# RMS norms of a two-layer backbone: squares added up as channel tiles finish, means by one-column matmuls inside the matmuls that follow

## The chip, the cores and the metric

The kernel runs on one core of one Trainium2 chip. The metric is the time of one execution on the device in microseconds, the median of several runs. A core has TensorE (PE, matmuls), VectorE (DVE), ScalarE (ACT), GpSimd (POOL) and SyncE (SP, which here only issues DMA transfers). Each engine takes its instructions in a fixed order and waits by semaphores for what the others make.

## What is computed

The reference is a backbone of two layers over 512 latent tokens and 256 context tokens with 1024 channels. A layer is

```
h = modulate(rms_norm(x, n1))                # per stream: latents, context
y = merge(conv(h), attention(h), deltanet(h))
x = x + gate1 * (y @ w_o)                    # output projection
h = modulate(rms_norm(x, n2))
x = x + gate2 * (convffn(h) @ f_dn)

rms_norm(x, g) = x * rsqrt(mean(x * x over channels) + 1e-6) * g
modulate(h)    = h * (1 + scale) + shift
```

Everything is float32. Only the latents are the output, so the last layer's context part stops early: its second norm and FFN are done for latents alone.

## The kernel before

Channels lie on partitions: a stream is eight tiles of 128 channels by its tokens, latents `l` with 512 columns and context `c` with 256. A mean over channels is therefore a sum over partitions and over eight tiles. Every large matmul is made of three products of exact high and low parts (`whi`, `wlo` for weights, `hl`/`ol` and `hc`/`oc` for modulated latents and context, `zhl`/`zol` and `zhc`/`zoc` for the merged branches). A weight unit (`wunit`, L140 to L152) is one DMA on SP's queue into one of two `raw` buffers, a cast to `whi` on ACT (L150) and a subtraction to `wlo` on DVE (L151); `ahead` prepares the next unit while one is used. A unit with eight channel tiles is 24 matmuls (`mm_b`, L169).

Eight norms are computed with `norm_stat` (L293 to L317): two at the start (before layer 0), latents' and context's second norm of layer 0 (behind `out_proj`), latents' and context's first norm of layer 1 (behind the last `down` of layer 0's FFN), and the second norm of layer 1, in two halves of 256 latents. For each of eight tiles ACT squares the tile (`sq`, L300) and PE multiplies the squares by a constant of 32 equal columns (`nps`, L302), four groups of 32 rows of a PSUM bank adding two tiles each. ACT copies the bank (`npe`, L304), four further matmuls add the groups and put a quarter of the tokens on each 32 rows (L307), DVE adds eps (`ms`, L310) and takes the reciprocal root in eleven operations (`_rsqrt`, L56 to L61: `nrt`, `nry`) on 128 or 64 columns, and four matmuls spread the result over all partitions (`nrb`, L314). `norm_apply` gives eight closures, one a channel tile: DVE scales (`nt`, L323), ACT adds the shift and rounds (L334), DVE makes the low part (L335).

In `out_proj` the loop runs over two parts (latents, then context; in the last layer two halves of latents) and in each over eight output tiles `m`; behind a tile's matmuls (`wo`) DVE adds the residual (`xml`, `xmc`, L1212) with a tile `xo` that is loaded through SP. The first part's norm is emitted behind its loop, and its eight closures are emitted one behind each tile of the second part's loop. While the first part runs, each tile emits instead a step of the modulation (`ada_steps`): loads of tables (`at`, SP, L262) and products on DVE (`aj`, L275). The last `down` of layer 0 is built in the same way, with residuals in `x`; the second part's norm and closures come behind the loop. The first unit of the FFN (`up(0)`) runs its three weight units over the first part and then over the second, so that the second part's norm can lie beside the first part's matmuls. Layer 1 begins with output-gate matmuls with tokens on the columns of the result (`og_proj`, L177, four groups of latents and then the context's 16 columns).

The order on each engine is set by a scheduler that walks the program in its order of emission, with pools of buffers (tags `t0` and `t1` have two buffers each; `sq`, `nt` and `aj` share `t1`) and with `issue_after`, which holds a closure behind a given instruction.

Of the kernel before, what the change touches and what calls it, by code (L numbers as in the profile page):

```python
# [31 lines left out]
# amounts of independent work emitted between dependent stages  # L32
# [3 lines left out]
# columns of the packed constants  # L36
# [3 lines left out]
# columns of the packed per-layer parameters  # L40
# [8 lines left out]
def _rsqrt(nc, sm, x, n, name):  # L49
    """1/sqrt(x) for a [128, n] tile: a seed from the exponent, then Newton steps to float32."""  # L50
# [14 lines left out]
class Net:  # L65
    def __init__(self, tc, A, out):
        self.tc, self.nc, self.A, self.out = tc, tc.nc, A, out
        self.queue, self.live, self.primed = deque(), None, None

    # ---------------------------------------------------------------- set-up  # L70
# [69 lines left out]
    # ---------------------------------------------------------------- weights  # L140
# [13 lines left out]
    def ahead(self, src, n, cols):  # L154
        """the weight units src(0) .. src(n - 1), each prepared while the one before is used"""
# [6 lines left out]
    def mm_b(self, outs, w, xs):  # L162
        """outs[s] = sum_k w(k).T @ xs[s][k], w and xs as exact (high, low) parts."""
        n = len(xs[0])
        for k in range(n):
            wk = w(k)
            for i, (a, b) in enumerate(((0, 0), (0, 1), (1, 0))):
                for o, x in zip(outs, xs):
                    self.nc.tensor.matmul(o, wk[a], x[k][b], start=(k == 0 and i == 0), stop=(k == n - 1 and i == 2))  # L169

    def mm_a(self, o, x, w):
        """o = sum_k x[k].T @ w(k), tokens on partitions."""
# [12 lines left out]
    # ---------------------------------------------------------------- adaLN  # L185
# [11 lines left out]
    def ada_rows(self):  # L197
        """silu(c) and silu(c_ctx) on every partition"""
# [88 lines left out]
    # ---------------------------------------------------------------- modulated RMSNorm  # L287
    def new_h(self, streams=(("l", NL), ("c", NX))):
        return {s: [self.pair_tiles(s, k) for k in range(8)] for s, _ in streams}

    def norm_stat(self, x, part):
        """1/rms of the tokens [a, b) of a stream, on every partition (a PSUM bank)"""
        nc, kc = self.nc, self.kc  # L293
        s, a, e = part
        n = e - a
        q = n // 4
        ps = self.bank("nps")
        for k in range(8):
            sq = self.tp.tile([128, 512], F32, tag="t1", name="sq")
            nc.scalar.activation(sq[:, :n], x[s][k][:, a:e], AF.Square)  # L300
            g = 32 * (k % 4)
            nc.tensor.matmul(ps[g:g + 32, :n], kc[:, K_S1024:K_S1024 + 32], sq[:, :n], start=k < 4, stop=k >= 4)  # L302
        pe = self.tp.tile([128, 512], F32, tag="t0", name="npe")
        nc.scalar.copy(pe[:, :n], ps[:, :n])  # L304
        p2 = self.bank("nps2")
        for g in range(4):
            nc.tensor.matmul(p2[32 * g:32 * g + 32, :q], kc[:, K_S32:K_S32 + 32], pe[:, q * g:q * g + q],  # L307
                             start=True, stop=True)
        ms = self.sm.tile([128, 128], F32, tag="ms", name="ms", bufs=1)
        nc.vector.tensor_scalar(ms[:, :q], p2[:, :q], EPS, None, ALU.add)  # L310
        r = _rsqrt(nc, self.sm, ms[:, :q], q, "nr")
        rb = self.bank("nrb")
        for g in range(4):
# [1100 lines left out]
```

## Time and profile before

| | us |
|---|---|
| median of 3 runs | 2627.74 |
| lowest, highest | 2625.46, 2634.8 |
| span of the profiled execution | 2622.8 |
| PE busy in it | 2530.2 (96%) |
| DVE busy | 1834.8 (70%) |
| ACT busy | 1071.1 (41%) |

The profile is one execution, with each instruction's start, its length, and the idle time of its engine before it with what ended that. Matmuls overlap in their pipeline, so two starts tell more than one length: the pace is the difference of starts. The granted clock (PEclk) is a share of TensorE's full speed. PE is near full all through the span, in 40 slices 9 tenths or more in all but the first and two others.

### The profile page before, as it was taken

How to read it: one execution, taken by the hardware profiler on the slowest of the kernel's cores; microseconds unless marked ns; L12 is line 12 of the kernel's file. 1: busy time of each engine (PE TensorE's matmuls, PEld its weight loads, DVE VectorE, ACT ScalarE, POOL GpSimd, SP SyncE). 2: the span in 40 equal slices, each digit the busy share in tenths (PEclk: the TensorE clock that was granted, in tenths of full speed). 3: DMA queues.
4: the chain of work that ended last, by engine and by line, in shares of the span. 5: the costliest groups of instructions: out<-in, count | busy, mean ns of one | idle time of the engine just before them, and what ended most of it. 6: DMA issues, size and time to landing. Idle time of an engine off the chain costs nothing. (4 is left out here: it accounts for less than half of the span.)

```text
span 2622.8 us, 42526 instructions
## 1 busy us (share of the span) xinstructions
PE 2530.2 (96%) x16247; PEld 2150.7 (82%) x16247; DVE 1834.8 (70%) x4082; ACT 1071.1 (41%) x2166; POOL 8.4 (0%) x32
## 2 busy tenths in 40 slices
PE   7999999999989999999999999998999999999999
PEld 3989888977878868888888788887887778888887
DVE  5676578789579968776656467776778976755463
ACT  3464343454332244223223345634354543533242
POOL 0000000000000000000000000000000000000000
PEclk8999999999999999999999999998999999999999
DMA  7224434352458643453432333343446375333332
GB/s 246 90 79 130 135 95 144 99 194 95 170 175 267 194 136 120 123 159 119 150 127 89 113 123 102 119 130 114 146 125 209 107 246 173 122 92 101 96 97 89
DMA packets 207276, 356.78 MB, mean 136 GB/s; under 512 B 54832, under 2 KB 103200, under 8 KB 206944
## 3 DMA queue, kind: packets, MB, share of 16 engines
q1 hardware_dynamic: 182176, 320.97, 39.1%
q10 hardware_dynamic: 24896, 33.09, 3.6%
q8 instruction: 128, 2.10, 0.3%
q14 instruction: 76, 0.62, 0.1%
HBM read 297.31 MB, written 56.68 MB: 135 GB/s over the span
## 5 line engine op out<-in xcount | busy, mean ns | idle before, releaser
L151 DVE TENSOR_TENSOR wlo<-raw,whi 128x1024 fp32r<-128x1024 f32 (+2 forms) x320 | 386.9, 1210 | 303.4 <-ACT whi L150 300.6
L150 ACT CAST whi<-raw 128x1024 fp32r<-128x1024 f32 (+2 forms) x320 | 332.5, 1040 | 626.5 <-PE dn L169 197.2
L169 PE MATMUL upl<-ol,whi 128*128 128x512 f32 (+1 forms) x728 | 282.3, 388 | 0.0
L169 PE MATMUL upl<-hl,whi 128*128 128x512 f32 (+1 forms) x728 | 282.1, 388 | 0.0
L169 PE MATMUL upl<-hl,wlo 128*128 128x512 f32 (+1 forms) x728 | 280.6, 386 | 0.7 <-DVE wlo L151 0.7
L454 PE MATMUL pjl<-hl,whi 128*128 128x512 f32 x512 | 210.9, 412 | 7.6 <-ACT whi L150 7.6
L525 DVE SCALAR_TENSOR_TENSOR ca<-yp,caw,ca 128x783 f32<-128x783 f32 (+1 forms) x240 | 213.0, 888 | 7.4 <-ACT ca L518 4.6
L454 PE MATMUL pjl<-hl,wlo 128*128 128x512 f32 x512 | 206.2, 403 | 0.9 <-DVE wlo L151 0.9
L454 PE MATMUL pjl<-ol,whi 128*128 128x512 f32 x512 | 206.2, 403 | 0.0
L169 PEld LDWEIGHTS upl<-ol,whi 128*128 128x128 f32 x728 | 136.8, 188 | 32.6 <-issue 2.1
L169 PEld LDWEIGHTS upl<-hl,wlo 128*128 128x128 f32 x728 | 136.8, 188 | 31.3 <-issue 1.2
L169 PEld LDWEIGHTS upl<-hl,whi 128*128 128x128 f32 x728 | 136.7, 188 | 29.1 <-issue 1.2
L169 PE MATMUL dn<-fhl,wlo 128*128 128x512 f32 x352 | 139.0, 395 | 0.0
L169 PE MATMUL dn<-fll,whi 128*128 128x512 f32 x352 | 139.0, 395 | 0.0
L169 PE MATMUL dn<-fhl,whi 128*128 128x512 f32 x352 | 138.6, 395 | 0.3 <-DVE xml L1280 0.3
L454 PEld LDWEIGHTS pjl<-hl,whi 128*128 128x128 f32 x512 | 97.7, 191 | 29.2 <-ACT whi L150 9.7
L275 DVE CUSTOM_DVE_ANT_1 aj<-at,crows,par 128x512 f32<-128x512 f32 x128 | 92.9, 749 | 34.1 <-DMA at<-ada_t 21.3
L454 PEld LDWEIGHTS pjl<-hl,wlo 128*128 128x128 f32 x512 | 97.5, 191 | 21.9 <-DVE wlo L151 1.6
L454 PEld LDWEIGHTS pjl<-ol,whi 128*128 128x128 f32 x512 | 98.2, 192 | 19.1 <-issue 0.5
L590 PE MATMUL na<-wlo,hl 128*128 128x256 f32 x384 | 108.8, 284 | 0.6 <-DVE wlo L151 0.6
L590 PE MATMUL na<-whi,hl 128*128 128x256 f32 x384 | 109.1, 285 | 0.0
L590 PE MATMUL na<-whi,ol 128*128 128x256 f32 x384 | 109.0, 284 | 0.0
(390 smaller groups left out, 6461.0 us busy)
## 6 DMA issues: line engine op xcount, KB each, us to landing
raw<-w_b SPq DMA_DIRECT2D x88, 512.0 KB
raw<-f_up SPq DMA_DIRECT2D x88, 512.0 KB
at<-ada_t SPq DMA_DIRECT2D x160, 256.0 KB
raw<-w_o SPq DMA_DIRECT2D x32, 512.0 KB
raw<-f_dn SPq DMA_DIRECT2D x32, 448.0 KB
raw<-w_a SPq DMA_DIRECT2D x24, 512.0 KB
mg<-mge ACTq DMA_DIRECT2D x48, 256.0 KB
raw<-w_br SPq DMA_DIRECT2D x24, 512.0 KB
```

The lines of the kernel that those rows point to most:

```text
L150: self.nc.scalar.copy(hi[:, :n], r[:, :n])
L151: self.split = self.nc.vector.tensor_sub(lo[:, :n], r[:, :n], hi[:, :n]).ins
L169: self.nc.tensor.matmul(o, wk[a], x[k][b], start=(k == 0 and i == 0), stop=(k == n - 1 and i == 2))
L275: V.tensor_tensor_reduce(p, w, self.crows[:, r, 4 * h:4 * h + 4], 1.0, m if h else self.p(l, "adab")[:, t:t + 1], ALU.mult, ALU.add, accum ...
L454: self.nc.tensor.matmul(o, wk[a], x[k][b], start=(k == 0 and i == 0), stop=(k == n - 1 and i == 2))
L525: nc.vector.scalar_tensor_tensor(a, y[:, k:k + n], w[:, 31 * c + k:31 * c + k + 1], a, ALU.mult, ALU.add)
L590: self.nc.tensor.matmul(ps[:, :256], x[k][a], wk[b], start=(k == 0 and j == 0), stop=(k == 7 and j == 2))
```

## The change

`norm_stat` is cut in pieces. `norm_open` takes a running tile `nac` for a part; `norm_add` squares a finished channel tile on ACT (the first square goes into `nac` itself) and adds it to `nac` on DVE (new line L306); it is called in the loops of `out_proj` and of the last `down`, right behind each tile's residual. `norm_mean` multiplies each block of 128 tokens of `nac`, as stationary operand, by one constant column (L314 after), so that a token's mean lands on its own partition, in one column for each block; eps and the reciprocal root then work on four or two columns. `norm_row` spreads them: a matmul for each block of 128 tokens, with a column of the root repeated 128 times as stationary operand and the identity as moving one (L324 after). The copy `npe` and the second step are gone.

The list of closures now holds the mean, then the spreading with the first two tiles, then six tiles. The first part's list is taken up one entry a tile in the second part's loop, as before. The second part's list is kept in `self.late`: `up(0)` emits the mean behind channel tile 6 of its first unit, the spreading behind tile 4 of the second, the rest behind tile 0 of the third (`mm_b` has a new argument `then`); in layer 1 `og_proj` emits the mean behind its first group and the rest behind its second, and the close of a pool (`zes`) has moved there from the layer's start. Every closure of `norm_apply` is still held behind `self.split`, now also when it is emitted late; mean and spreading are not. Comments and docstrings are gone too.

```
+    def norm_open(self, part):
+        n = part[2] - part[1]
+        return {"n": n, "k": 0, "acc": self.tp.tile([128, 512], F32, tag="t0", name="nac")[:, :n]}
+
+    def norm_add(self, st, x):
+        nc, n = self.nc, st["n"]
+        if st["k"] == 0:
+            nc.scalar.activation(st["acc"], x, AF.Square)
+        else:
+            sq = self.tp.tile([128, 512], F32, tag="t1", name="sq")[:, :n]
+            nc.scalar.activation(sq, x, AF.Square)
+            nc.vector.tensor_add(st["acc"], st["acc"], sq)
+        st["k"] += 1
+
+    def norm_mean(self, st):
+        nc, nt = self.nc, st["n"] // 128
+        ps = self.bank("nps")
+        for t in range(nt):
+            nc.tensor.matmul(ps[:, t:t + 1], st["acc"][:, 128 * t:128 * t + 128], self.kc[:, K_S1024:K_S1024 + 1],
+                             start=True, stop=True)
+        ms = self.sm.tile([128, 4], F32, tag="ms", name="ms")
+        nc.vector.tensor_scalar(ms[:, :nt], ps[:, :nt], EPS, None, ALU.add)
+        st["r"] = _rsqrt(nc, self.sm, ms[:, :nt], nt, "nr")
+
+    def norm_row(self, st):
+        rb = self.bank("nrb")
+        for t in range(st["n"] // 128):
+            self.nc.tensor.matmul(rb[:, 128 * t:128 * t + 128], st["r"][:, t:t + 1].to_broadcast([128, 128]), self.ident,
+                                  start=True, stop=True)
+        st["rb"] = rb
...
-    def norm_apply(self, l, x, h, part, rb, gain, shift):
+    def norm_apply(self, l, x, h, part, st, gain, shift):
...
+        def head():
+            self.norm_row(st)
+            one(0)
+            one(1)
+
+        return [lambda: self.norm_mean(st), head] + [lambda k=k: one(k) for k in range(2, 8)]
...
@@ og_proj
+                if i == 0 and t == 2:
+                    for f in self.late[:1]:
+                        f()
+                elif i == 0 and t == 3:
+                    for f in self.late[1:]:
+                        f()
+                    self.zes.close()
...
@@ out_proj, in the loop over m
+                self.norm_add(st, self.x[s][m][:, a:e])
...
-            late = self.norm_apply(l, self.x, self.h, part, self.norm_stat(self.x, part), g2, 3)
-        for f in late:
-            f()
+            late = self.norm_apply(l, self.x, self.h, part, st, g2, 3)
+        self.late = late
...
@@ up(0)
+                    mean, head, *rest = self.late
+                    then = [{6: mean}, {4: head}, {0: lambda: [f() for f in rest]}]
                     for part in self.parts():
                         for u in us:
-                            self.up_mm(*u, [part])
+                            self.up_mm(*u, [part], then.pop(0) if then else {})
...
@@ the last down
-                        down(k0, k1, hid, [p], self.xsrc, late)
-                        late = self.norm_apply(l + 1, self.x, self.h, p, self.norm_stat(self.x, p), g1, 0)
-                    for f in late:
-                        f()
+                        st = self.norm_open(p)
+                        down(k0, k1, hid, [p], self.xsrc, late, st)
+                        late = self.norm_apply(l + 1, self.x, self.h, p, st, g1, 0)
+                    self.late = late
```

On PE, at the end of layer 0's latent output projection and the beginning of the context's, the order before is (`wo` is the projection's bank, 128x512 its latent matmuls, 128x256 the context's; `nps` is the sum of squares):

```order
L169 MATMUL wo<-zhl_9889,wlo 128x512
L302 MATMUL nps<-sq,kc 32x512 x2
L169 MATMUL wo<-zhc_9893,whi 128x256
L169 MATMUL wo<-zoc_9894,whi 128x256
L169 MATMUL wo<-zhc_9893,wlo 128x256
L169 MATMUL wo<-zhc_9897,whi 128x256
L169 MATMUL wo<-zoc_9898,whi 128x256
L169 MATMUL wo<-zhc_9897,wlo 128x256
L302 MATMUL nps<-sq,kc 32x512
L169 MATMUL wo<-zhc_9901,whi 128x256
```

The same place after, at the end of the context's first unit (its first two rows there follow the last latent matmul):

```order
L169 MATMUL wo<-zhl_9877,wlo 128x512
L169 MATMUL wo<-zhc_9881,whi 128x256
...
L169 MATMUL wo<-zhc_9909,whi 128x256
L169 MATMUL wo<-zoc_9910,whi 128x256
L169 MATMUL wo<-zhc_9909,wlo 128x256
L314 MATMUL nps<-kc,nac 128x1 x4
L169 MATMUL wo<-zhc_9881,whi 128x256
L169 MATMUL wo<-zoc_9882,whi 128x256
```

The eight matmuls on squares, which were spread over the first 25 matmuls of the context's projection, are gone, and four one-column matmuls stand behind its first 24.

On DVE, around the last latent residual of layer 0's output projection (`xml`), the order before is (`aj` are the modulation's products, `mc` their sums, `wlo` the low weights, `ms` the norm's sum with eps, `nrt` and `nry` its root):

```order
L151 TENSOR_TENSOR wlo<-raw,whi 128x1024
L1212 SCALAR_TENSOR_TENSOR xml_9934<-wo,m_9925,xo 128x512
L151 TENSOR_TENSOR wlo<-raw,whi 128x1024
L1212 SCALAR_TENSOR_TENSOR xmc_9935<-wo,m_9925,xo 128x256
L151 TENSOR_TENSOR wlo<-raw,whi 128x1024
L310 TENSOR_SCALAR ms<-nps_10384 128x128
L56 TENSOR_SCALAR nrt<-ms 128x128
L57 TENSOR_SCALAR nry<-nrt 128x128
L59 TENSOR_TENSOR nrt<-nry 128x128
L1212 SCALAR_TENSOR_TENSOR xmc_9936<-wo,m_9925,xo 128x256
```

and after, with the second products of each pair left out:

```order
L151 TENSOR_TENSOR wlo<-raw,whi 128x1024
L1242 SCALAR_TENSOR_TENSOR xml_9922<-wo,m_9913,xo 128x512
L277 ISA aj,mc_84<-at,crows,par 128x512
...
L306 TENSOR_TENSOR nac<-nac,sq 128x512
...
L277 ISA aj,mc_84<-at,crows,mc_84 128x512
...
L1242 SCALAR_TENSOR_TENSOR xmc_9923<-wo,m_9913,xo 128x256
L317 TENSOR_SCALAR ms<-nps 128x4
L151 TENSOR_TENSOR wlo<-raw,whi 128x1024
L277 ISA aj,mc_84<-at,crows,par 128x512
...
L277 ISA aj,mc_84<-at,crows,mc_84 128x512
...
L56 TENSOR_SCALAR nrt<-ms 128x4
```

Eight products and one addition now stand behind the last latent residual: four products around the addition, and four between the sum and its root.

On PE in layer 1's output projection, where the second half of the latents begins, the order after is:

```order
L169 MATMUL wo<-zhl_23050,wlo 128x256
L169 MATMUL wo<-zhl_23022,whi 128x256
L314 MATMUL nps<-kc,nac 128x1 x2
L169 MATMUL wo<-zol_23023,whi 128x256
L169 MATMUL wo<-zhl_23022,wlo 128x256
```

The row ahead of these is the end of the second half's first unit; the mean of the first half stands behind the first matmul of the second unit, where before the squares of the first half stood in six places from the beginning of that half on.

## Rows read from the trace of the kernel before

**Rows 1.** The page's first part: busy time, share of the span, instructions.

```profile
PE 2530.2 (96%) x16247; PEld 2150.7 (82%) x16247; DVE 1834.8 (70%) x4082; ACT 1071.1 (41%) x2166; POOL 8.4 (0%) x32
```

**Rows 2.** Windows (PE and PEld busy, PEclk, DMA share) of L302; sums of L307, L314.

```profile
0.00:60.00 60.00, 11.41 (x32) 2.28 (x32) 0.83 0.74 258
900.00:1010.00 110.00, 11.55 (x32) 2.18 (x32) 1.00 0.48 149
1480.00:1600.00 120.00, 10.74 (x32) 1.92 (x32) 1.00 0.39 124
2180.00:2280.00 100.00, 8.54 (x32) 1.92 (x32) 0.98 0.44 140
...
sum 390.00, PE 2.87 PEld 1.26; mean PE 0.72 PEld 0.31
...
sum 390.00, PE 10.51 PEld 9.37; mean PE 2.63 PEld 2.34
```

**Rows 3.** Timeline of PE, layer 0's norm2: start, length, instruction, [idle before <-releaser].

```profile
927.68 0.39 PE L169 MATMUL wo<-zhl,wlo 128*128 128x512 f32 x1
...
931.06 0.28 PE L169 MATMUL wo<-zoc,whi 128*128 128x256 f32 x1
931.18 0.28 PE L169 MATMUL wo<-zhc,wlo 128*128 128x256 f32 x1
931.39 1.04 PE L302 MATMUL nps<-sq,kc 128*32 128x512 f32 x2
932.37 0.39 PE L169 MATMUL wo<-zhc,whi 128*128 128x256 f32 x1
...
960.49 0.39 PE L169 MATMUL wo<-zhc,wlo 128*128 128x256 f32 x1 [1.39 <-DVE wlo L151]
...
986.96 0.28 PE L169 MATMUL upc<-hc,whi 128*128 128x256 f32 x1
```

**Rows 4.** One line's instructions, L1181: count, shortest/median/longest ns, first and last.

```profile
L1181 DVE TENSOR_TENSOR zc<-zc,mth x16: 417/427/433, 825.4 to 885.3; 128x256 f32<-128x256 f32 x16
```

**Rows 5.** The same view of lines L247 and L275.

```profile
L247 DVE TENSOR_REDUCE mc<-ada x4: 182/192/192, 23.5 to 49.0; 128x8 f32<-128x32 f32 x4
...
L275 DVE CUSTOM_DVE_ANT_1 aj<-at,crows,par x128: 740/748/762, 713.4 to 1403.1; 128x512 f32<-128x512 f32 x128
```

**Rows 6.** Timeline of DVE, layer 0's norm2.

```profile
938.44 0.48 DVE L1212 SCALAR_TENSOR_TENSOR xmc<-wo,m,xo 128x256 f32<-128x256 f32 x1 [6.73 <-PE wo L169]
...
950.95 0.48 DVE L1212 SCALAR_TENSOR_TENSOR xmc<-wo,m,xo 128x256 f32<-128x256 f32 x1
951.35 1.22 DVE L151 TENSOR_TENSOR wlo<-raw,whi 128x1024 fp32r<-128x1024 f32 x1
952.48 1.41 DVE L335 SCALAR_TENSOR_TENSOR ol<-nt,mc,hl 128x512 fp32r<-128x512 f32 x2
```

**Rows 7.** Timeline of PE, layer 1's norm1.

```profile
1505.12 0.39 PE L169 MATMUL dn<-fhl,wlo 128*128 128x512 f32 x1
...
1536.37 0.38 PE L169 MATMUL dn<-fhc,wlo 128*128 128x256 f32 x1 [1.51 <-DVE wlo L151]
...
1559.07 0.17 PE L177 MATMUL og<-whi,hc 128*128 128x16 f32 x1
```

**Rows 8.** Timeline of ACT and PE, layer 1's norm2, the first half's squares.

```profile
2218.13 1.04 ACT L150 CAST whi<-raw 128x1024 fp32r<-128x1024 f32 x1 [3.14 <-DMA raw<-w_o]
...
2219.55 0.77 PE L302 MATMUL nps<-sq,kc 128*32 128x256 f32 x2 [3.24 <-ACT sq L300]
```

**Rows 9.** Windows behind that: busy PE, PEld, DVE, ACT, POOL, PEclk, DMA share, GB/s.

```profile
2220.00:2224.00 4.00, 4.00 (x15) 1.96 (x15) 0.43 (x1) 1.10 (x3) 0.00 (x0) 0.59 0.46 139
```

**Rows 10.** Timeline of PE at the start: the spreading of both norms.

```profile
18.23 2.06 PE L314 MATMUL nrb<-nry,kc 128*128 128x128 f32 x8 [3.01 <-DVE nry L61]
...
32.47 1.94 PE L314 MATMUL nrb<-nry,kc 128*128 128x64 f32 x8 [2.40 <-DVE nry L61]
```

**Rows 11.** Windows at the start, columns as in rows 9.

```profile
30.00:35.00 5.00, 2.60 (x12) 1.98 (x14) 2.52 (x11) 0.00 (x0) 0.00 (x0) 0.69 1.05 387
```

More of the change, by code (lines that the diff above doesn't have):

```diff
@@ L67, in __init__ @@
         self.tc, self.nc, self.A, self.out = tc, tc.nc, A, out
-        self.queue, self.live, self.primed = deque(), None, None
+        self.queue, self.live, self.primed, self.late = deque(), None, None, []
     def run(self):
@@ L160, in ahead, with mm_b @@
             w = v
-    def mm_b(self, outs, w, xs):
+    def mm_b(self, outs, w, xs, then={}):
         n = len(xs[0])
@@ L169, in mm_b @@
                     self.nc.tensor.matmul(o, wk[a], x[k][b], start=(k == 0 and i == 0), stop=(k == n - 1 and i == 2))
+            if k in then:
+                then[k]()
     def mm_a(self, o, x, w):
@@ L291, in norm_stat @@
+    def norm_row(self, st):
[4 more added lines that the diff above has]
+        st["rb"] = rb
     def norm_stat(self, x, part):
-        nc, kc = self.nc, self.kc
         s, a, e = part
-        n = e - a
-        q = n // 4
-        ps = self.bank("nps")
+        st = self.norm_open(part)
@@ L298, in norm_stat @@
         for k in range(8):
[L299 to L313, printed above, removed]
-            nc.tensor.matmul(rb[:, q * g:q * g + q], self.ident[:, 32 * g:32 * g + 1].to_broadcast([128, 128]), r,
-                             start=True, stop=True)
-        return rb
+            self.norm_add(st, x[s][k][:, a:e])
+        self.norm_mean(st)
@@ L335, in norm_shift @@
             nc.vector.scalar_tensor_tensor(lo[:, a:e], t[s][k][:, a:e], sh, hi.bitcast(F32)[:, a:e], ALU.add, ALU.subtract)
-    def norm_apply(self, l, x, h, part, rb, gain, shift):
+    def norm_apply(self, l, x, h, part, st, gain, shift):
         s = part[0]
         def one(k):
-            t = {s: {k: self.tp.tile([128, 512], F32, tag="t1", name="nt")[:, :x[s][k].shape[1]]}}
-            self.norm_scale(t, x, part, rb, gain, k, k + 1)
-            self.norm_shift(l, t, h, part, shift, k, k + 1)
-        def gated(k):
             with self.tc.issue_after(self.split):
-                one(k)
-        return [lambda k=k: gated(k) for k in range(8)]
+                t = {s: {k: self.tp.tile([128, 512], F32, tag="t1", name="nt")[:, :x[s][k].shape[1]]}}
+                self.norm_scale(t, x, part, st["rb"], gain, k, k + 1)
+                self.norm_shift(l, t, h, part, shift, k, k + 1)
+        def head():
+            self.norm_row(st)
+            one(0)
+            one(1)
+        return [lambda: self.norm_mean(st), head] + [lambda k=k: one(k) for k in range(2, 8)]
     def layer(self, l):
@@ L1205, in out_proj @@
             r_ = 0 if s == "l" else 1
+            st = self.norm_open(part)
             for m, (hi, lo) in self.ahead(lambda m: self.A["w_o"][l, m], 8, 1024):
@@ L1270, in up, with down @@
                 return res + [conv(NFF + i, us[1][1], "v")]
-            def down(k0, k1, hid, parts, after=None, late=()):
+            def down(k0, k1, hid, parts, after=None, late=(), st=None):
                 for m, (hi, lo) in self.ahead(lambda m: self.A["f_dn"][l, m, :, k0:k1, :], 8, 128 * (k1 - k0)):
@@ L1312, in ffn, with up_mm @@
                     for p in whole:
-                        down(k0, k1, hid, [p], self.xsrc, late)
-                        late = self.norm_apply(l + 1, self.x, self.h, p, self.norm_stat(self.x, p), g1, 0)
-                    for f in late:
-                        f()
-    def up_mm(self, w, ps, parts):
+                        st = self.norm_open(p)
+                        down(k0, k1, hid, [p], self.xsrc, late, st)
+                        late = self.norm_apply(l + 1, self.x, self.h, p, st, g1, 0)
+                    self.late = late
+    def up_mm(self, w, ps, parts, then={}):
         hi, lo = w
         self.mm_b([ps[s][:, a:e] for s, a, e in parts], lambda k: (hi[:, 128 * k:128 * k + 128], lo[:, 128 * k:128 * k + 128]),
-                  [[(u[:, a:e], v[:, a:e]) for u, v in self.h[s]] for s, a, e in parts])
+                  [[(u[:, a:e], v[:, a:e]) for u, v in self.h[s]] for s, a, e in parts], then)
 def _consts():
```

4 lines of the change are left out of this document (3 added, 1 removed).

## The prediction

> **What bounds the kernel now.** I read the busy shares first: TensorE (PE) is busy 96% of a span of 2622.8 us, VectorE (DVE) 70%, ScalarE (ACT) 41% [rows 1]. Work that leaves PE in a dense stretch therefore shortens the run, unless another engine becomes the last one there. Second, the windows of the four stretches that hold the eight norms, with the old norm's matmuls alone [rows 2]: the sums of squares (L302) take 11.41, 11.55, 10.74 and 8.54 us of PE, the second step (L307) 2.87 in all, the spreading of 1/rms (L314) 10.51 in all. The first two go, 45.1 us; the third stays in kind. Third, the timelines of PE and DVE in each stretch, since busy time is not yet loss. The span stands 4.9 us under the median of 2627.74; I take that rest as unchanged and subtract gains from the median.
>
> **What a norm costs on PE.** One place in full, in layer 0's norm2: a projection matmul starts at 931.18, the norm's at 931.39, the next projection matmul at 932.37 [rows 3]. That is 1.19 us from start to start where 0.12 is the pace, so 1.07 is lost for a busy time of 1.04. In a dense stretch the busy time of L302 is therefore the loss, give or take 0.3. With a quarter of L307 (0.72) a stretch of two norms loses 12.3, 11.5 and 9.3 us in the three that are dense, and what PE waits for the norm besides.
>
> **What the new form costs on PE.** One-column matmuls aren't in the trace. Bounds for the means of one part: from below L307 (2.87 / 8 = 0.36 for four), from above L314 (10.51 / 8 = 1.3 for four) [rows 2]. Their stationary side is as wide as L314's, their moving side narrower than L307's; I take 0.6 for four and 0.4 for two, nearer to L307, so 1.0 a stretch, between 0.6 and 2. The spreading has one matmul for 128 columns: for 512 tokens four as before, for 256 two in place of four, which may save up to 0.5; I count nothing.
>
> **What moves to DVE, and where it binds.** Squares stay on ACT, one a tile; its copy of the sums goes. New on DVE are seven additions a part. An addition of this kind takes 0.43 us for 256 columns [rows 4], some 0.36 where one follows another; for 512 it is at most a modulation product's 0.75 [rows 5], in latent units that last 5.6 us on PE (24 at twice the pace). The root's twelve steps shrink from 128 or 64 columns to 4 or 2; an 8-column operation takes 0.19 [rows 5].
>
> *Layer 0, norm2.* The context unit is 24 matmuls at just under 0.12 (931.06 to 931.18 [rows 3]), some 2.8 us of PE. DVE has per unit the low weights 1.13 (start of L151 to the next), the residual 0.40, a latent scaling 0.66 and a low part 0.66 (half of a pair's 1.41, less the overlap) [rows 6]: 2.85. With the addition it is 3.2. So DVE becomes the last engine there, and 8 x 0.4 = 3.2 us go back. The order adds more: eight modulation products that stood before the last latent residual now stand behind it, four of them between the mean (ms) and the rest of its root. At 0.67 (0.75 each [rows 5], less the overlap) they are 5.4 us, against 6.7 us in which DVE stood idle before 938.44 [rows 6]; I let 2.5 of them show as a wait of PE on low weights, between none and all. Before, PE already had 1.39 us of that wait at 960.49 [rows 3]; 1.2 of it is in these sums twice and is credited. The wait on a square ahead of the first place, some 0.7, goes. Gain: 12.3 + 0.7 - 1.0 - 3.2 - 2.5 + 1.2 = **7.5** (4 to 10).
>
> *Layer 1, norm1.* No modulation products stand here, and the context's norm has moved behind the second and third group of output-gate matmuls, which don't need it. PE waited 1.51 us at 1536.37 on low weights that norm work had delayed [rows 7]. Bottom up: 11.5 + 1.5 - 1.0, and for DVE's excess, 8 x 0.35 = 2.8, less: 9.2. By the order: the stretch from 1505.36 (a pace behind the last latent matmul) to 1559.07, where the 16-column matmuls start, lasts 53.7 us [rows 7]; after, it is eight context units at 3.25 (DVE's pace, 26.0), 96 gate matmuls of 272 columns at 0.125, 272/256 of 0.118 (12.0), 1.2 for mean and spreading and about 1 of stalls, 40.2, a gain of 13.5. I take **12**, nearer to the order's sum, which counts every instruction that stands there (9 to 13.5).
>
> *Layer 1, norm2.* Both halves have 256 columns. PE stood 3.24 us at 2219.55 for a square that was queued on ACT behind a weight cast, which waited for its DMA, and then ran at a mean granted clock of 0.59 for 4 us [rows 8, 9], between the two levels of 1.2 and 2.4 GHz. So 9.3 + 3.2, less 0.8 for the means. DVE has room here (1.13 + three at 0.40 + 0.36 = 2.7 a unit). But the mean waits for the last addition, which the order has put behind the low weights of that late cast; some 2.2 us of the 3.24 stay, with some of the slow clock. 9.3 + 3.2 - 0.8 - 2.2 - 0.5 = **9** (6 to 11).
>
> *The start.* PE waits here, so what counts is the chain: 3.01 us for the latent root before 18.23 and 2.40 for the context's before 32.47 [rows 10]. After, the latent spreading can start some 2.6 us sooner (no copy, no second step, a root of about 2.2 us; more by the mean and one addition), the context's another 1.7. But the DMA engines are at 1.05 of their share until 35 us [rows 11], and the modulation's weights, which come next, pass through them: **4** (0 to 6.5).
>
> Sum: 4 + 7.5 + 12 + 9 = 32.5; 2627.7 - 32.5 = **2595**. The ends give 19 to 41, 2587 to 2609.
>
> **Rivals.** *PE alone counts* (D). All 45.1 us come back, with the 3.2 and 1.5 of waits, less 3.8 for the means of three parts of 512 and five of 256 tokens: 46, but the start's 11.4 are worth 6.5 at most: 41, 2587. For it: 96% on PE; against it: DVE's 3.2 us over PE's 2.8 in two of the stretches [rows 6]. The Trainium skill (Perfetto Trace Analysis, Identifying the Most-Contended Engine) has one optimize the engine with the highest occupancy first, which is this rival; its Optimization Strategy adds that the most contended engine can change from stage to stage, as the rows of the context unit show it here.
>
> *DVE and its loads take the bound* (A). If the eight products all lie on the path (5.4) and weight loads wait on SP's queue behind the four loads of modulation tables that now stand among the context's weights (one unit, 2.8 us, in all), layer 0's norm2 gives 2 at most; layer 1's norm1 then 9, its norm2 6, the start 0: 17 down to 15, so 2612. For it: the products fill DVE in that stretch already; against it: the 6.7 us of idle DVE.
>
> *The loads hold the ends* (B). The start gives 0, layer 1's norm2 only 4, since its weights come 3 us late from DMA whatever the norm does: 7.5 + 12 + 4 = 23.5, 2604. For it: [rows 8, 11]; against it: half of that stretch's 8.5 us came with no such wait.
>
> *PE waits for every sum* (C), slower. PE takes its work in order; a mean that comes before its sum, or a spreading before its root, stops all behind it. The price of one stop is in the trace: 3.24 us, then 4 us at 0.59, 1.6 lost, together 4.9 [rows 8, 9]. Six norms stand in dense matmuls. One stop each is 29, the gain just cancelled; two each, at the mean and at the spreading, are 59 - 32.5 = 26, 2654. It decides from 5.4 us per norm. For it: the new order puts weight preparations of 1.2 us, and products, on DVE between the last tile and its sum. Against it: a mean has at least 21 matmuls of cover (2.5 us) for a residual, a square and an addition of at most 0.75 each, and only one part of six had a late cast. The Trainium skill (TensorE: Matmul & The Clock Gate, HAM oscillation) says that matmul bursts broken by waits for data fall back to the half clock; the clock behind 2219.55 agrees with it.
>
> *The change doesn't do what it says*: the means could stand at their old places. The order shows the first 24 matmuls behind the last tile and no 32-row matmul left; no chance of its own.
>
> **How the numbers follow.** Forecast 0.62, D 0.10, A 0.13, B 0.11, C 0.04. A measurement tells 0.5%, 13 us, from no change: 2614.6 is the edge. Forecast, D and B lie under it, A by two chances in three: faster 0.88, same 0.09, slower 0.03. The range takes D's end and A's: 2586 to 2613.
>
> **What would show it.** Right: in the profile after, no 128*32 matmuls in the three dense stretches; from the last latent matmul of layer 0's projection to the first context matmul of the FFN, 927.92 to 986.96 or 59.0 us before [rows 3], about 51.5; norm1's stretch of 53.7 down to about 41; in layer 1's norm2 a PE wait of about 2 us on the sum. Wrong: PE waiting on low weights for over 8 us in one stretch (A); an idle of over 3 us and a clock near 0.5 behind a mean or a spreading in each norm (C); 3 us of wait on the weights' DMA in the last norm and a start that ends where it did (B). An FFN or attention stretch elsewhere that changes by over 2 us would be a cause that I don't have.

## The result, and the profile after

The changed kernel takes 2598.58 us (median of 4 runs, 2592.68 to 2599.55); the kernel before, run beside it, 2628.42 (4 runs). The ratio is 0.9886 with an interval of 0.9863 to 0.9909: faster by 29.8 us, where 32.5 were forecast. Run again later the ratio is 0.9909 (0.9876 to 0.9941), so about 0.990 is what is known, some 26 us.

The profile's first part gives span and busy times of the kernel after:

```profile
span 2590.9 us, 42262 instructions
PE 2495.3 (96%) x16079; PEld 2154.6 (83%) x16079; DVE 1853.1 (72%) x4138; ACT 1068.0 (41%) x2158; POOL 8.4 (0%) x32
```

PE is busy 34.9 us less than in [rows 1] and the span is 31.9 us shorter, while DVE has 18.3 us more and still only 72%. The time went where PE's work went. By stage, from the starts of the PE rows of the profiled executions (us; "after" and "after again" are two profiles of one kernel, and the range in the last column tells by how much two executions of identical code differ):

| stretch | before | after | after again | gain forecast | gain |
|---|---|---|---|---|---|
| layer 0, norm2: last latent `wo` to first `upc` | 59.3 | 49.9 | 48.7 | 7.5 | 9.4 to 10.6 |
| layer 1, norm1: last latent `dn` to first 16-column `og` | 53.9 | 38.3 | 38.6 | 12 | 15.3 to 15.6 |
| `og`: first 16-column matmul to last `og` | 17.9 | 24.2 | 24.2 | none | -6.3 |
| layer 1, norm2: first `wo` to first 512-column `upl` | 80.7 | 70.1 | 72.6 | 9 | 8.1 to 10.6 |

By these profiles the three stages won 34 to 36 us where the forecast had 28.5, and the `og` stretch, which had none in it, gave 6.3 back. Two lengths of before are not typical, though. One is the 17.9 us of `og`, of which more below. The other is 80.7: in the four other profiles with the old form at the last norm (of the runs below) this stretch takes 77.1 to 79.1 us, and in the seven with the new form 69.1 to 72.7. By the means of these five and seven, 78.3 and 71.1, the last norm gains about 7 us. The same means are 60.1 and 49.9 for layer 0's norm2, 53.9 and 38.5 for norm1.

**Layer 0, norm2.** PE's timeline of the kernel after (start, length, engine, line, operation, count, and the idle time before with what ended it):

```profile
922.39 0.40 PE L169 MATMUL wo<-zhl,wlo 128*128 128x512 f32 x1
...
925.33 0.28 PE L169 MATMUL wo<-zhc,wlo 128*128 128x256 f32 x1
925.44 0.95 PE L314 MATMUL nps<-kc,nac 128*128 128x1 f32 x8
926.25 0.37 PE L169 MATMUL wo<-zhc,whi 128*128 128x256 f32 x1
...
933.97 0.39 PE L169 MATMUL wo<-zhc,wlo 128*128 128x256 f32 x1 [1.60 <-DVE wlo L151]
937.51 1.14 PE L324 MATMUL nrb<-kc,nry 128*128 128x128 f32 x8
944.73 0.39 PE L169 MATMUL wo<-zhc,whi 128*128 128x256 f32 x1 [0.98 <-ACT whi L150]
945.61 0.39 PE L169 MATMUL wo<-zhc,wlo 128*128 128x256 f32 x1 [0.36 <-DVE wlo L151]
950.52 0.79 PE L169 MATMUL upl<-hl,whi 128*128 128x512 f32 x1 [2.07 <-ACT whi L150]
...
959.57 0.50 PE L314 MATMUL nps<-kc,nac 128*128 128x1 f32 x4
965.77 0.68 PE L324 MATMUL nrb<-kc,nry 128*128 128x128 f32 x4
...
972.25 0.28 PE L169 MATMUL upc<-hc,whi 128*128 128x256 f32 x1
```

The stretch is 922.39 to 972.25, 49.9 us. The mean of four blocks takes 925.33 to 926.25, 0.92 from start to start where 0.12 is the pace: 0.8 lost, with no wait for the sum. The context's mean and spreading (959.57, 965.77) have half as many rows as the latents'. The waits listed are 1.60, 0.98, 0.36 and 2.07 us, 5.0 in all, each on a weight's cast or low part: DVE and ACT are late there. (Six other profiles with the new form here have 3.6 to 6.7.) DVE's timeline, from the first wait to behind the last:

```profile
927.59 1.22 DVE L151 TENSOR_TENSOR wlo<-raw,whi 128x1024 fp32r<-128x1024 f32 x1
929.00 0.75 DVE L277 CUSTOM_DVE_ANT_1 aj<-at,crows,par 128x512 f32<-128x512 f32 x1 [0.19 <-DMA at<-ada_t]
...
932.70 1.22 DVE L151 TENSOR_TENSOR wlo<-raw,whi 128x1024 fp32r<-128x1024 f32 x1
...
952.54 1.22 DVE L151 TENSOR_TENSOR wlo<-raw,whi 128x1024 fp32r<-128x1024 f32 x1
...
954.33 0.43 DVE L306 TENSOR_TENSOR nac<-nac,sq 128x256 f32<-128x256 f32 x1
954.67 0.75 DVE L343 SCALAR_TENSOR_TENSOR nt<-xml,gain,nrb 128x512 f32<-128x512 f32 x1
...
955.72 1.23 DVE L151 TENSOR_TENSOR wlo<-raw,whi 128x1024 fp32r<-128x1024 f32 x1
```

The first wait, 1.60 us at 933.97, ends with the low part of 932.70, which stands behind four of the moved products; from the low part before it are 5.1 us. The low parts behind it begin at 934.78, 938.96, 944.33 and 949.35, the last three some 5 us apart, and between those DVE is hardly idle: it catches up with scalings, `ol` rows and additions. Late low parts make late loads and casts too, since the next load waits until a low part has freed its buffer (SP waits 14.8 us for that, in seven loads between 922 and 958 us). Only behind the last wait, where PE has begun the FFN, do they come 955.72 - 952.54 = 3.18 us apart, with no idle time. That is the 3.2 per context unit of the prediction, with 0.34 of it the new addition (954.33 to 954.67), but at a place where PE doesn't wait for them.

**Layer 1, norm1.** PE after:

```profile
1489.78 0.40 PE L169 MATMUL dn<-fhl,wlo 128*128 128x512 f32 x1
...
1492.94 1.05 PE L314 MATMUL nps<-kc,nac 128*128 128x1 f32 x8
1497.96 1.16 PE L324 MATMUL nrb<-kc,nry 128*128 128x128 f32 x8
...
1514.86 0.29 PE L179 MATMUL og<-whi,hl 128*128 128x272 f32 x1
...
1519.56 0.54 PE L314 MATMUL nps<-kc,nac 128*128 128x1 f32 x4
1525.59 0.71 PE L324 MATMUL nrb<-kc,nry 128*128 128x128 f32 x4
...
1528.03 0.17 PE L179 MATMUL og<-whi,hc 128*128 128x16 f32 x1
```

No row of the stretch, shown or left out, has an idle time. From 1490.02 (a pace behind the last latent matmul) to 1514.86 are 24.84 us; less about 2 for the mean and the spreading that is 2.85 a context unit, PE's own pace and not DVE's. DVE's low parts in the same place:

```profile
1501.92 1.23 DVE L151 TENSOR_TENSOR wlo<-raw,whi 128x1024 fp32r<-128x1024 f32 x1
...
1505.11 1.22 DVE L151 TENSOR_TENSOR wlo<-raw,whi 128x1024 fp32r<-128x1024 f32 x1
...
1508.29 1.22 DVE L151 TENSOR_TENSOR wlo<-raw,whi 128x1024 fp32r<-128x1024 f32 x1
...
1511.48 1.28 DVE L151 TENSOR_TENSOR wlo<-raw,whi 128x1088 fp32r<-128x1088 f32 x1
```

They come 3.2 us apart, slower than PE's 2.85, but only from the latents' spreading on, and the last of them, ready at 1512.76, is first used at 1514.98. DVE began with a lead and had 2.2 us of it left.

**Layer 1, norm2.** PE after, at the first half's mean:

```profile
2198.15 0.58 PE L314 MATMUL nps<-kc,nac 128*128 128x1 f32 x4 [2.02 <-DVE nac L306]
2200.08 0.41 PE L169 MATMUL wo<-zhl,whi 128*128 128x256 f32 x1
2200.29 0.41 PE L169 MATMUL wo<-zol,whi 128*128 128x256 f32 x1
```

The wait of [rows 8] is there in its new form, 2.02 us on the sum, and behind it projection matmuls go at 0.21 us, the half clock, until about 2203. It is the one mean in a dense stretch that waited. But the 3.24 us of [rows 8] are the longest of five such waits. In the four other profiles with the old form it is 1.3 to 1.8 us, here with the new form at layer 0's norm2 alone:

```profile
2220.18 0.62 PE L339 MATMUL nps<-sq,kc 128*32 128x256 f32 x2 [1.66 <-ACT sq L337]
```

In the seven with the new form it is 1.9 to 2.7 us. So the wait has not become shorter, and the gain of this stretch is PE's work.

**The start.** PE's timeline, and ACT's row of the first modulated latents, after and before:

```profile
15.95 2.07 PE L324 MATMUL nrb<-kc,nry 128*128 128x128 f32 x8 [0.59 <-DVE nry L61]
...
29.60 1.01 PE L314 MATMUL nps<-kc,nac 128*128 128x1 f32 x4 [5.66 <-DVE nac L306]
...
33.03 1.22 PE L324 MATMUL nrb<-kc,nry 128*128 128x128 f32 x4 [0.58 <-DVE nry L61]
```

```profile
38.45 2.56 ACT L354 ACTIVATE hl<-xl,mc 128x512 fp32r<-128x512 f32 x4 [1.70 <-DVE mc L250]
```

```profile
38.61 2.56 ACT L334 ACTIVATE hl<-xl,mc 128x512 fp32r<-128x512 f32 x4 [1.70 <-DVE mc L248]
```

The latents' spreading begins 2.28 us sooner than the row at 18.23 of [rows 10]; the context's begins at 33.03 against 32.47. The first modulated latents start at 38.45 for 38.61 before. Only 0.16 us of the start's gain reaches the next stage.

### The profile page after: what moved, and what is told of

It is laid out like the page before. It is cut to its first block, busy times and chain, and to the rows that moved or that the text cites. A ratio compares the mean times of both kernels' runs of the same rounds, so it can differ in the third digit from the quotient of the medians.

```text
span 2590.9 us, 42262 instructions
## 1 busy us (share of the span) xinstructions
PE 2495.3 (96%) x16079; PEld 2154.6 (83%) x16079; DVE 1853.1 (72%) x4138; ACT 1068.0 (41%) x2158; POOL 8.4 (0%) x32
## 5 line engine op out<-in xcount | busy, mean ns | idle before, releaser
L169 PEld LDWEIGHTS upl<-ol,whi 128*128 128x128 f32 x728 | 136.8, 188 | 29.8
```

## Experiments: one norm at a time

Kernels that have the old norm at some places and the new one, in its new place, at others. With a flag for the start, layer 0's norm2, layer 1's norm1 and layer 1's norm2, the edit is one line, here for the first of four (of the others each has its own 1):

```
-NEW = (1, 1, 1, 1)
+NEW = (1, 0, 0, 0)
```

The start alone:

> The new form at the start alone, the other six norms as before. Theory 'the start is held by the loads': the first 16-column results of the output gate (db) come 0 to 2 us sooner than before's 60.04, hl of the first modulated tiles still near 38.5; total 0 to -2 us, 2626 to 2628. Rival 'the chain counts', as forecast: 4 us sooner, total 2624.

Layer 0's norm2 alone:

> The new form behind layer 0's output projection alone. Theory 'PE's own work': from the last latent matmul of that projection to the first context matmul of the FFN 49.9 us as in the changed kernel (59.3 before), total -9.4, 2619. Rival 'the stretches help each other' (the earlier weight loads of one stretch are what shortens the next): under 6 us here, total over 2622.

Layer 1's norm1 alone:

> The new form behind layer 0's last down alone (layer 1's norm1). Theory 'the clock gives back': from the last latent matmul to the first 16-column matmul 38.3 us (53.95 before), then a PE wait of about 1 us on a weight cast among 16-column matmuls and some 12 us at a granted clock of 0.50; net -9, total 2619. Rival 'the low clock there was chance': the clock stays at 1.00 behind the 16-column matmuls and the whole 15.7 us arrive, total 2612.

Layer 1's norm2 alone:

> The new form behind layer 1's output projection alone. Theory 'PE's own work': from that projection's first matmul to the first 512-column matmul of the FFN 70.1 us as in the changed kernel (80.7 before), with a PE wait of 2 us on the running sum; total -10.6, 2618. Rival 'the stretches help each other': under 7 us, total over 2621.

All on one chip, against 2630.58 us for the kernel before (28 runs):

| new norm at | median us | ratio (95%) | whole, us | its stretch, us |
|---|---|---|---|---|
| start | 2639.72 | 1.0032 (1.0018 to 1.0045) | +9.1 | about none |
| layer 0, norm2 | 2623.48 | 0.9972 (0.9954 to 0.9991) | -7.1 | 59.3 to 49.8, -9.5 |
| layer 1, norm1 | 2616.73 | 0.9952 (0.9933 to 0.9972) | -13.9 | 53.9 to 38.3, -15.6 |
| layer 1, norm2 | 2621.47 | 0.9971 (0.9956 to 0.9987) | -9.1 | 80.7 to 71.8, -8.9 |

Each dense norm gives what the forecast gave it (7.5, 12, 9) within its interval, which is 8 to 10 us wide; together 30.1. Totals with such intervals don't part the theories of these expectations: two of them, 2623.48 and 2621.47, lie on the side of 'the stretches help each other'. The stretches say more. Those of layer 0's norm2 and of norm1 are as short alone as in the full change; the last norm's 71.8 is 8.9 under before's profile and 5 to 7 under the four others with the old form. Behind norm1 the clock falls as its theory had it (`og` 24.2). The start fits neither of its theories: it makes the kernel slower, which no case of the prediction held.

To see whether these add, all but the start, beside a second run of the full change:

```
-NEW = (1, 1, 1, 1)
+NEW = (0, 1, 1, 1)
```

> The changed kernel with the two norms of the start in the old form. Theory 'the new start costs' (the start alone came out 8 us above before): 8 us under the changed kernel. Rival 'the start is worth nothing, and the 8 us were the granted clock's other turns in stretches that both share': within 3 us of the changed kernel.

> The changed kernel again, beside its variants on the same chip. All theories: -30 us against before, 0.9886; the low clock among layer 1's 16-column output-gate matmuls is there or not as in five of the six profiles so far, since the kernels with the old norm showed it too.

Without the start 2596.25 us, ratio 0.988 (0.9851 to 0.9909), 29.6 less than before: the sum of the three is 30.1, so they add as far as an interval of 15 us can tell. The full change beside it, 2603.03 us. The start's price by this pair is 6.8 us, which the run of the start alone allows (4.7 to 11.8), but the two intervals of the pair overlap. So the start was run alone once more, on another chip:

> The new form at the start alone, once more, since 8 us more than before had no place in its trace. Theory 'the new start costs, in the clock or elsewhere': again 5 to 11 us above before. Rival 'the granted clock's turns': within 4 us of before.

2638.79 us against 2629.36, ratio 1.0038 (1.0017 to 1.0059): +9.4. The loss repeats.

**Where the start's loss lies.** Not in the start: the first copy of the next stage (`db` on DVE) comes at 59.7 and 59.0 us in the two profiles with the new start alone, at 60.0 before and between 58.5 and 63.2 in others with the old one. The code behind it is the same, yet in layer 0's DeltaNet DVE waits in one and not in the other. The row that begins its chains, before, with the new start alone, after, and with all but the start:

```profile
225.47 3.24 DVE L788 SCALAR_TENSOR_TENSOR D<-D,G,km 128x128 f32<-128x128 f32 x12
```

```profile
227.03 3.24 DVE L855 SCALAR_TENSOR_TENSOR D<-D,G,km 128x128 f32<-128x128 f32 x12 [2.23 <-DMA D<-row]
```

```profile
225.59 3.24 DVE L817 SCALAR_TENSOR_TENSOR D<-D,G,km 128x128 f32<-128x128 f32 x12 [2.13 <-DMA D<-row]
```

```profile
223.77 3.24 DVE L855 SCALAR_TENSOR_TENSOR D<-D,G,km 128x128 f32<-128x128 f32 x12
```

With the new start there is a wait on the load of a row from DMA, with the old one none, under old dense norms and new. So it is in every profile of this case: the seven with the new form at the start wait 1.9 to 2.3 us here, the seven with the old form don't. Between 202 and 299 us the kernels with the new start lose 2 to 4 us against before, those with the old start at most 0.1. (In three of the seven, DVE waits another 1.75 us on ACT near 243 us.)

The row's load is late because SP issues it late. SP waits there until the transfer `tokk<-tok`, which ACT issued, has landed. SP's waits between 205 and 224 us, before and with the new start alone (in all, times, longest):

```profile
SPq L785 <- DMA tokk<-tok: 11.4, 1, 11.4
```

```profile
SPq L852 <- DMA tokk<-tok: 13.7, 1, 13.7
```

From the issue of `tokk<-tok` to that of the row's load are 2.5 us in the seven kernels with the old start and 4.4 to 5.1 us in the seven with the new. A transfer's end is told in 16 parts. With the old start the last part of `tokk<-tok` comes within 0.05 us of the fifteenth, with the new 1.8 to 2.6 us behind it.

The traces' DMA records show what lies beside it. One queue carries packets of 16384 bytes, of a kind that the profile calls instruction, here before:

```profile
q8 instruction: 128, 2.10, 0.3%
```

One of them starts every 254 matmuls and weight loads of PE (the median), so they are most likely PE's own code. The new start has 40 matmuls fewer, 80 such instructions with their weight loads, and so the program has moved against the loading of its code: with the old start a packet begins 4.2 to 4.8 us ahead of the issue of `tokk<-tok`, with the new 1.0 to 2.3 us behind it, seven profiles against seven. Nor is it this transfer alone. In four profiles (before, the new start alone, after, all but the start) the last part comes over 0.5 us behind the fifteenth in 44 of 81 transfers that land while such a packet is under way or up to 0.8 us behind it, and in 27 of 904 others, counted over transfers whose first fifteen parts land within 0.3 us.

So: that the new start costs some 9 us when it is alone is shown, and that 2 to 4 of them lie at this wait too. That a load of code which now falls on another transfer makes the wait fits every profile, but no kernel was run that moves the code and leaves the start as it was. Where the rest lies is open. Up to the first matmul of layer 0's output projection the seven profiles with the old start come in at 882.5 to 884.9 us, the seven with the new one at 877.6 (the full change) to 893.7 (with the doubled additions of a run below): not only later in the mean, but spread far wider.

## Experiments: the form or the place

The change does two things to a dense norm: PE's 32-row sums become additions on DVE, and means and spreadings are emitted among later matmuls. First the new form at the old place, mean, spreading and closures all emitted right behind the loop:

```
-        return [lambda: self.norm_mean(st), head] + [lambda k=k: one(k) for k in range(2, 8)]
+        self.norm_mean(st)
+        self.norm_row(st)
+        return [lambda k=k: one(k) for k in range(8)]
```

and the late list taken up at once, with no `then` in `up(0)` and none in `og_proj`.

> The changed kernel, but mean, root, spreading and closures are emitted right behind each part's loop, as the old norm was, and nothing is handed on to the FFN or the output gate. Theory 'the form is the gain': the same within 4 us, since the order puts the means at the same places within 4 matmuls. Rival 'the place is the gain': over 10 us of the 30 lost, PE waits for the running sum in front of each mean.

2602.97 us, ratio 0.9898 (0.9864 to 0.9931), the same as the change beside it (2603.03); the stretches are 49.4, 39.0 and 70.9 us, with two waits of 0.6 us on the running sum. But this says less of the place than its name: in the order of this kernel the means stand within four matmuls of where the change has them, since the scheduler fills PE with matmuls that are ready whichever line emits the norm.

Then the old sums at the new place: the squares go to PE again, 32 rows of a bank, tile by tile, and the second step is back, with a root on 128 or 64 columns.

```
-            nc.vector.tensor_add(st["acc"], st["acc"], sq)
+        nc.tensor.matmul(st["ps"][g:g + 32, :n], self.kc[:, K_S1024:K_S1024 + 32], sq, start=k < 4, stop=k >= 4)
```

> The changed kernel's placing (each tile squared as it finishes, mean and spreading handed on), but with the old sums: 32-row matmuls on the squares, copy, second step, the root on 128 or 64 columns. Theory 'the form is the gain', PE's time: L302's 8 to 12 us a stretch are back; 57 to 60 us in layer 0's norm2 (49.8 in the changed kernel, 59.5 before), 48 to 53 in norm1 (38.4, 53.9), 77 to 80 in layer 1's norm2 (71, 78.5); total 2620 to 2628. Rival 'the place is the gain': within 10 us of the changed kernel.

2629.72 us, ratio 1.0001 (0.9985 to 1.0018): the whole gain is gone, though its start, with the old sums too, doesn't carry the new start's loss (nor its wait at 227 us). Its stretches are 51.9, 44.8 and 77.4, the first two shorter than expected. PE's timeline ahead of the last latent matmul of norm1 (1513.88) tells why:

```profile
1481.90 1.04 PE L304 MATMUL nps<-sq,kc 128*32 128x512 f32 x2
...
1488.67 1.05 PE L304 MATMUL nps<-sq,kc 128*32 128x512 f32 x2
```

Tile by tile, a sum of 1.04 us stands in each latent unit, ahead of the point from which the stretch is measured. Seven of them, 7.3 us, make 59.2 and 52.1 of the two: the expectation of longer ones had overlooked where the measured stretch begins. The sums cost PE the same wherever they stand. The gain is the form: taking them from PE.

**DVE's share.** Each addition doubled, into the tile of squares, which is dead by then:

```
             nc.vector.tensor_add(st["acc"], st["acc"], sq)
+            nc.vector.tensor_add(sq, st["acc"], sq)
```

> The changed kernel with a second addition of the same size behind each addition (into the square's tile, which nobody reads afterwards). Theory 'DVE is the last engine in the context units': 7 x 0.36 us more in layer 0's norm2 and in norm1, each 2 to 4 us longer, layer 1's norm2 up to 1; 5 to 8 us in all. Rival 'DVE has room': within 1.5 us in each stretch.

2614.05 us, ratio 0.9938 (0.9918 to 0.9959), against 0.9886 and 0.9909 for the change: 8 to 14 us dearer by the ratios, though its interval overlaps that of the second. Norm1 goes from 38.3 to 41.4, norm2 of layer 1 from 70.1 and 72.6 to 73.6; layer 0's norm2 doesn't move (49.3). In norm1 PE now waits where it did not, 0.59 and 0.41 us on low weights at the end of the context units and 0.33 twice at the gate's first matmuls: one more addition, 0.34 us a unit, used up the 2.2 us of lead. That agrees with DVE at the edge there, not over it: the theory holds for norm1, the rival for layer 0's norm2. The rest of the 8 to 14 us lies in no dense norm's stretch. The start's additions are doubled too, and this profile is the latest of all at the first matmul of layer 0's projection (893.7 us), but one profile doesn't place the rest.

## Experiments: the output gate's clock

The `og` stretch is longer after by 6.3 us, with the same matmuls. Windows of the profile there, kernel after (stretch, its length, PE's busy time and instructions, PEld, DVE, ACT and POOL likewise, the granted clock, the DMA share and GB/s):

```profile
1530.00:1535.00 5.00, 3.87 (x32) 3.77 (x31) 3.00 (x7) 1.86 (x3) 0.00 (x0) 0.92 0.00 0
1535.00:1540.00 5.00, 5.00 (x26) 5.00 (x25) 2.24 (x6) 0.91 (x2) 0.00 (x0) 0.50 0.36 131
1540.00:1545.00 5.00, 5.00 (x25) 5.00 (x25) 1.74 (x8) 1.44 (x2) 0.00 (x0) 0.50 0.00 0
...
1550.00:1555.00 5.00, 5.00 (x37) 4.58 (x36) 4.09 (x13) 3.73 (x7) 0.00 (x0) 1.00 0.20 53
```

From 1535 to 1545 PE is busy all the time at 0.50, the level of 1.2 GHz. A wait of 1.13 us on high weights at 1533.33 stands ahead of it, and could be its cause. The other suspects are the matmuls of 16 columns, 48 of which come here in two groups. They were made as wide as the others, at the price of columns that nobody reads:

```
-                        self.mm_a(ps[:, 256:272], self.htok(t), lambda k: w(k, 256, 272))
+                        self.mm_a(ps[:, :wd], self.htok(t), w)
```

> The changed kernel with layer 1's context output-gate matmuls made over all 272 columns of the weight instead of the 16 that are used (48 matmuls, 0.11 to 0.125 us each, 0.7 us more work). Theory 'narrow matmuls let the clock fall': granted clock 1.00 from the second to the last gate matmul, 5 us less than the changed kernel. Rival 'the wait on a weight cast lets it fall': clock 0.50 for 12 us as before, 0.7 us more.

2597.97 us, ratio 0.9878 (0.9846 to 0.9911), 5.1 under the change beside it, with intervals that overlap. The stretch is 17.5 us in place of 24.2, and the clock, in windows of PE alone, is full:

```profile
1545.00:1550.00 5.00, 5.00 (x42) 1.00 0.42 131
1550.00:1555.00 5.00, 5.00 (x44) 1.00 0.44 126
```

The wait is not needed for the fall. With the new start alone, where norm1 is old and no PE row from the first narrow matmul on has an idle time before it, the same windows of PE read:

```profile
1560.00:1565.00 5.00, 5.00 (x44) 1.00 0.21 74
1565.00:1570.00 5.00, 5.00 (x32) 0.71 0.07 23
1570.00:1575.00 5.00, 5.00 (x26) 0.50 0.44 134
```

Over all profiles of this case: 12 with narrow matmuls, 10 of which fall to 0.50 there (`og` 22 to 25 us, under old norms and new) and 2 don't (before, and all but the start: 17.9 and 18.0); 2 with wide ones, which don't (17.5 both). Nor is the wait enough for the fall: all but the start has the same 1.13 us among its narrow matmuls, and stays at 1.00. So in these profiles the fall at this place comes with the narrow matmuls only, and the change didn't make it; the two wide profiles are few, and why 2 of 12 narrow ones escape is not known. That the profile of before is one of the two made the table above look worse by 6 us. Whether the timed runs of before have the fall isn't shown, but their clock gives a hint: the mean granted clock of a whole execution is 0.978 to 0.983 in the ten profiles that fall and 0.984 to 0.987 in the four that don't, and of 57 timed runs of before 37 have 0.983 or less.

Last, both repairs at once, the old start and the wide gate:

```
-NEW = (1, 1, 1, 1)
+NEW = (0, 1, 1, 1)
...
-                        self.mm_a(ps[:, 256:272], self.htok(t), lambda k: w(k, 256, 272))
+                        self.mm_a(ps[:, :wd], self.htok(t), w)
```

> The changed kernel with the start's two norms in the old form and the context's output-gate matmuls over 272 columns: the two that came out lowest, together. If both gains are real, 10 to 13 us under the changed kernel, 2586 to 2592 beside 2628 before; if only the wide matmuls' is, 5 under it; if neither, the same.

2591.63 us (5 runs, 2588.8 to 2598.68) against 2629.36: ratio 0.9867 (0.9845 to 0.9889). It is the lowest of all kernels here and 37.7 us under before. It lies 7 to 11 us under the change by medians; the intervals of the ratios overlap, so that it beats the change is likely, not shown. Against the wide gate with the new start (0.9878) it is 0.0011 or 3 us lower, with overlapping intervals: within the full change the start's price is 3 to 8 us by two pairs, neither of them clear of noise.

## Why the prediction was right, and where it was not

**Direction and time: right**, 2598.6 (2603.0 again) for 2595. But the closeness is in part luck. By whole times the three stages won 30 us where 28.5 were written, by the means of their stretches 33; and the start, alone, took 9 where 4 were to come. The two errors offset each other in part, and the first of the two measurements, 29.8, lies above the second, some 24. (The chances as written give 0.62 + 0.10 + 0.11 + two thirds of 0.13 = 0.92 for faster, not 0.88.)

**PE's busy time in a dense stretch is the loss: right.** With the sums back on PE the gain is nil, and the three norms add up (30.1 from single runs, 29.6 together).

**Means and spreadings: right in size for the mean.** Four columns cost 0.8 us where 0.6 was taken, inside 0.36 and 1.3, and five of the six means in dense stretches come without a stop. The context's spreading of two matmuls takes 0.68 against the latents' 1.14: 0.46 saved, the "up to 0.5" that was not counted.

**Layer 0, norm2: 7.5 forecast, some 9.5 measured.** Both terms of waiting are near: 1.60 us behind the moved products for 2.5, and 0.98 + 0.36 + 2.07 = 3.4 on DVE's and ACT's lateness for 3.2, though not at an even pace of 3.2 us a unit. The 2 us more are small terms. Some 1.7 are waits: PE waited 2.9 us here before (four waits, of which the forecast credited two in part) and 5.0 after, 2.1 more, where 3.8 were charged. The context's spreading gives 0.46.

**Layer 1, norm1: 12 forecast, 15.6 measured.** The terms that failed are "eight context units at 3.25 (DVE's pace, 26.0)" and the "about 1 of stalls". A slower engine costs nothing until its lead is used up: DVE fell back some 0.35 us a unit over three or four units, from a lead of which 2.2 us remained. PE ran at 2.85, so 8 x 0.4 = 3.2 of those terms were not there, nor the stalls. Against that, the "1.2 for mean and spreading" was too small. From start to start, two means and two spreadings lose some 3 us, so the order's sum of 40.2 came out at 38.0. The doubled addition shows how near the edge DVE was.

**Layer 1, norm2: 9 forecast, 8.1 to 10.6 measured against the one profile of before, about 7 against the mean of five.** The wait on the sum came as written, 2.02 us for 2.2, with the half clock behind it. But the 3.2 us that the forecast got back for the old wait rest on one execution: the others had 1.3 to 1.8, so there was nothing to win from the wait, and the agreement of 9 with the table is luck in part.

**The start: 4 forecast, 9 lost when alone.** Two steps failed. One was that the chain's gain would arrive: the latents' spreading is 2.28 us sooner, but the context's squares on ACT now wait for DVE's additions, its mean waits 5.66 us, and the modulation's weights set the end as they did; rival B had that half. The other was that nothing behind the start would move: the text itself said that a change of over 2 us elsewhere would be a cause that it lacked, and this is one, at 227 us.

**The rivals.** D's first half was nearer than thought (PE alone counts in norm1), its time of 2587 not. A fell: 3.6 to 6.7 us of waits in layer 0's stretch, not over 8. B was right at the start, wrong at the last norm, where 7 came for its 4. C stands at one place, the one named, and at no other. That the means keep their place: the run of the new form at the old place shows that it would have changed nothing measurable.

## What to carry to other kernels

A sum over tiles that is taken on the bounding engine is worth moving whole to one with room, and the price is that engine's pace only once its lead is gone: follow both from the first unit of the stretch on. Test each place of a change alone when it is made at several; here one of four places cost 9 us when it was run alone, beside the 30 that the others won, and a right total hid it. Compare a stretch's length, waits and granted clock in several profiles of each form before a difference is put down to an edit: the one profile of before was some 5 us short in one stretch here and 3 us long in another.

## What was not expected of the hardware

- TensorE's clock fell to 0.50 in a stretch in which PE was busy 5.00 of 5.00 us, during matmuls of 16 columns, in 10 of 12 profiles; with 272 columns in their place it stayed at 1.00 in both and the stretch took 17.5 us for 24. The Trainium skill (TensorE: Matmul & The Clock Gate, HAM oscillation) puts such falls down to bursts broken by waits for data; in the kernel with the new start alone no such wait stands among these matmuls, and the trace doesn't agree there.
- The 16-column matmuls are hardly cheaper at full clock: the stretch takes 17.9 and 18.0 us with them, waits of 0.44 and 1.13 us included, and 17.5 with 272 columns in their place and no wait.
- An edit at 5 to 35 us goes with a DMA wait of 1.9 to 2.3 us near 227 us, in code that is the same on every engine: 7 profiles of 7, against none of 7 without the edit. Beside it a 16384-byte packet of code begins 1.0 to 2.3 us behind the issue of the transfer that is waited for, where without the edit it begins 4.2 to 4.8 us ahead; the last of that transfer's 16 parts lands 1.8 to 2.6 us behind the others, where without the edit it is within 0.05 us.
